# A decoder trunk on one core: pairs of gate/up blocks in seven products, in another form of the seven, and with a second pair in three of the four FFNs

## The chip, the cores and the metric

The kernel runs on one core of a Trainium2 chip. The metric is the device time of one execution in microseconds (us). The kernel before was timed three times: 978.38, 978.43 and 982.04 us, median 978.43.

## The reference, cut to what matters

Two layers work on x, 256 rows of 1024 numbers, in float32. Each layer has an FFN, a mixer (mLSTM beside attention to a memory in the first layer, dilated attention beside it in the second), and another FFN. Between the layers one projection makes keys and values that the second layer uses. The change is in the four FFNs:

```python
D_MODEL, SEQ, DEPTH, D_FF = 1024, 256, 2, 2816
def swiglu(h, w_gate, w_up, w_down):
    return (jax.nn.silu(h @ w_gate) * (h @ w_up)) @ w_down
...
    x = x + 0.5 * swiglu(rms_norm(x, ffn1_norm[layer]), ffn1_w_gate[layer], ffn1_w_up[layer], ffn1_w_down[layer])
    ...
    x = x + mix
    x = x + 0.5 * swiglu(rms_norm(x, ffn2_norm[layer]), ffn2_w_gate[layer], ffn2_w_up[layer], ffn2_w_down[layer])
```

The four FFNs are named here by layer and place: (0,1), (0,2), (1,1), (1,2).

## The kernel before, in words

**Numbers in two parts.** Every float32 operand of a matmul is split into a high and a low part: ScalarE (ACT) rounds it (`hi`), VectorE (DVE) subtracts that from it (`lo`). `mm3` (line 797) then issues three matmuls in place of one: x high by w low, x high by w high, x low by w high. So every unit of weights, a tile of 128x1024 numbers, costs a load of 512 KB, one rounding on ACT and one subtraction on DVE before TensorE (PE) can use it. `emit_unit` (line 658) issues that; the split weights go into a ring of 8 tiles each (`RING`, tags `hi` and `lo`), in the order in which PE uses them. Weights come in one packed array by the SP queue, into 6 buffers (`RAW`).

**An FFN in blocks.** The 2816 hidden columns are 11 blocks of 256. `gu(b, t)` makes gate and up of block b for the row half t (128 rows): 8 slices of 128 input channels, three matmuls of 128x512 each, so 24 matmuls in one PSUM bank (pool `mm`, two banks). `activated` (line 1030) makes silu on ACT and the product on DVE. For nearly all blocks `hidden_blocks` then transposes 32x32 squares on DVE, and `placed` (line 1066) sends the block through DRAM (`hd` out, `ht` back, one `ht` buffer) to put the squares where they belong, and splits it (`hhb`, `hlb`). `dn(b, t)` multiplies it with two units of w_down into the accumulators: 12 matmuls for each t.

**Pairs in seven products.** One pair of blocks, 5 and 6, is made in each FFN otherwise. Two row halves, two halves of the input channels and two blocks form a 2x2 product of matrices, which has eight block products; with sums of blocks on both sides seven are enough. `seventh(b, m)` (line 1163) issues product m: four channel slices, so 12 matmuls, with two units (k = 0 and 2). The sums of x are made once in an FFN (`sums`, line 1135) into the tiles `th` and `tl`. The sums of weights are made for every pair, in three buffers a, b and c for each k (`SLOTS`, line 75, `next_part`, line 620, `remade`, line 638): three subtractions or additions on DVE for each k, and two more as adding transfers, which a queue of GpSimd (POOL) issues and which add the next part of the weights into the buffer in SBUF. The results are put together from PSUM in the tiles `e` and `g`, with one copy on ACT and six sums on DVE of 128x512.

**The order of the work** is written out by hand in `PLANS` (line 49), one string for an FFN: g4 is `gu` of block 4, d2 is `dn` of block 2, 57 is product 5 of the pair that begins with block 7 (the product first, then the block), and p stands for a unit of the second mixer's output weights that is loaded, split and stored ahead of time in DRAM. Behind the string come `gu` of block 10 and the `dn` that the string left out, rows of t = 0 first: `gu(10,0)`, `dn` of the first block left, `gu(10,1)`, and so on (the end of `ffn_in`). In (0,1) and (1,1) the projection of the memory stands behind g4. PE runs in this order. The instructions of the other engines are put in order when the program is built, by a model of the engines (`_Model`, line 251; `until`, line 514): a chain's next step, or the split of the next unit, is written when the model's clock says that its inputs are ready. On the chip the engines' queues are then fixed, and each runs in order.

Of the kernel before, what the change touches and what calls it, by code (L numbers as in the profile page):

```python
# [12 lines left out]
ALU = mybir.AluOpType  # L13
# [27 lines left out]
def turned(layer, which, b):  # L41
# [20 lines left out]
SEVEN = {2: (2, 3), 5: (1, 0), 4: (3,), 3: (0,), 1: (0, 3), 6: (2, 0), 7: (1, 3)}  # L62
# [4 lines left out]
TWICE = ((0, 1), (0, 2), (1, 2))  # L67
# [5 lines left out]
PARTS = ((2, 0), (2, 2), (5, 0), (5, 2), (4, 0), (4, 2))  # L73
LAST = {"a": (1, 3, 4), "b": (6,), "c": (7,)}
SLOTS = {2: ("a", (0,), None), 5: ("b", (3,), None), 4: ("c", (2, 0), None),
         3: ("b", (1,), 5), 1: ("a", (), 5), 6: ("b", (), 3), 7: ("c", (), 4)}
# [33 lines left out]
def _stream():  # L110
# [26 lines left out]
    def ffn(layer, which):  # L137
# [11 lines left out]
        def st(b, m):  # L149
            for k in (0, 2):  # L150
                parts = tuple((layer, which, b, i, k) for i in SLOTS[m][1])
                units.append((("st", layer, which, b, m, k), ("parts", layer, parts, k, 2), 1024))
# [281 lines left out]
class _Kernel:  # L434
# [141 lines left out]


# [13 lines left out]
    def begin_parts(self, layer, which, plan, pool):  # L591

        self.partp, self.slots = pool, {}
        self.twice = (layer, which) in TWICE
        self.pairs = [(layer, which, s[1]) for s in plan if s[0] == "st" and s[2] == 2]
        self.todo = [(p, m, k) for p in range(len(self.pairs)) for m, k in PARTS]

    def before_part(self):

        p, m, k = self.todo[0]  # L600
        slot = SLOTS[m][0]
        p -= 2 if slot == "a" and self.twice else 1
        return [] if p < 0 else [(self.pairs[p], i, k) for i in LAST[slot]]

    def part_ready(self):
# [3 lines left out]
        p, m, k = self.todo[0]  # L609
        if self.index[("st",) + self.pairs[p] + (2, 0)] > self.next + EARLIER:  # L610
            return False
        if SLOTS[m][0] == "b" and not self.summed:
            return False
# [3 lines left out]
        return self.index[("st",) + self.pairs[p] + (m, k)] <= self.next + SOON or \  # L617
            self.model.clock["sync"] < self.now + LEAD

    def next_part(self):  # L620

        p, m, k = self.todo.pop(0)
        slot, parts, _ = SLOTS[m]
        if slot == "a" and (not self.twice or p % 2 == (self.pairs[p][:2] == (0, 1))):
            t = self.work.tile([P, 1024], F32, tag="mem", name="pa")
        else:
            t = self.partp.tile([P, 1024], F32, tag=f"p{slot}{k}", name=f"p{slot}{k}")
        pair = self.pairs[p]
        self.slots[pair, slot, k] = t
# [8 lines left out]
    def remade(self, pair, m, k):  # L638

        nc = self.nc  # L640
# [17 lines left out]
    def emit_unit(self):  # L658
# [12 lines left out]
        def steps(raw):  # L671
# [6 lines left out]
            if src[0] == "parts" and SLOTS[key[4]][2]:  # L678
                yield from self.wait(self.made[key[1:4], SLOTS[key[4]][2], key[5]])
# [30 lines left out]
        if src is not None and src[0] == "parts":  # L710
            slot = key[1:4], SLOTS[key[4]][0], key[5]
            while slot not in self.slots:
                self.finish(*[self.made[c] for c in self.before_part()])
                self.next_part()
            self.raw[i] = self.slots[slot]
# [28 lines left out]
    def unit_ready(self):  # L744
# [12 lines left out]
        if key[0] == "st" and SLOTS[key[4]][2]:  # L757
            c = self.made.get((key[1:4], SLOTS[key[4]][2], key[5]))
            if c is None or not c.done:
                return 1e9  # L760
        at = max(model.ready(raw[:, :self.units[i][2]]),
# [56 lines left out]
    def rms(self, src, out, later=LATER):  # L818
# [5 lines left out]
        for h in range(2):  # L824
            junk = self.work.tile([P, 512], BF16, tag="junk", name="junk")
# [188 lines left out]
    def ffn_in(self, layer, which, after, memory, fp):  # L1014
# [120 lines left out]
        def sums():  # L1135
# [4 lines left out]
            for t in range(2):  # L1140
                xs.append(fp.tile([P, NK, P], F32, tag=f"pb{2 * t}", name="xs"))
# [11 lines left out]
            for m in taken:  # L1153
                x, d = SEVEN[m], part[SEVEN[m][0]]
                if len(x) > 1:
                    d = self.work.tile([P, 4, P], F32, tag="sq", name="xd")
                    nc.vector.tensor_tensor(d, part[x[0]], part[x[1]], ALU.subtract)
                    yield
                yield from self.split(*taken[m], d)
# [864 lines left out]
```

## Time and profile before

| | |
|---|---|
| Profiled execution | 979.42 us, span 977.7 us, granted clock 1.0 |
| Median of the three timed runs | 978.43 us |
| PE, matmuls | 968.5 us busy (99%), 4631 instructions |
| PE, weight loads (PEld) | 805.4 us (82%) |
| DVE | 741.2 us (76%) |
| ACT | 580.0 us (59%) |
| POOL | 60.3 us (6%) |
| DMA | 220.79 MB, 226 GB/s; the adding transfers are 16 of 512 KB |

PE's busy share is made with modelled ends of pipelined matmuls, so it cannot tell how much of the time PE really works; the distance from one start to the next can. In the views, tiles are named as in the code: `gups` is the PSUM bank of a gate/up block or of a product, `acc` that of `dn`, `lo<-raw,hi` is the subtraction of a split, `pa`, `pb` and `pc` are the buffers of a pair's weights. Line 369 is the helper that issues every instruction of ACT, DVE, POOL and SP; line 787 is every matmul. The four FFNs lie at about 5 to 199, 319 to 498, 533 to 723 and 786 to 977 us of the span, the first mixer at 199 to 319, the keys and values at 498 to 533, and the second mixer at 723 to 786.

### The profile page before, as it was taken

To read this page: it belongs to the slowest core of one execution; us is meant where nothing else is said; L and a number is where in the kernel's file an instruction comes from. 1 tells how busy PE (TensorE), PEld (TensorE's weight loads), DVE (VectorE), ACT (ScalarE), POOL (GpSimd) and SP (SyncE) were. 2 spreads that over 40 slices of the span, in tenths; PEclk is the share of its full clock that TensorE was granted. 3 is DMA by queue.
4 is the path that set the end of the run, shared out by engine and by line. 5 is a ranking of instruction groups with operands and counts; after the bars stand their busy time and mean duration, and the time that the engine had idled before them with its cause. 6 is when DMAs were issued, how large, how long until landed. Compare 5 with 4: busy or idle time off the path is not lost.

```text
span 977.7 us, 13188 instructions
## 1 busy us (share of the span) xinstructions
PE 968.5 (99%) x4631; PEld 805.4 (82%) x4631; DVE 741.2 (76%) x1097; ACT 580.0 (59%) x921; POOL 60.3 (6%) x94
## 2 busy tenths in 40 slices
PE   9999999999999999999999999999999999999998
PEld 6787888899998888888888888888887788888887
DVE  5986985569886789965676897987676778689653
ACT  7766564477665655654476576575565585556541
POOL 0003000010010001000012002000012000000000
PEclk9999999999999999999999999999999999999999
DMA  9998398346355689588655889769658247965751
GB/s 357 321 331 251 89 313 267 99 148 226 122 193 197 224 257 264 166 258 290 215 180 186 273 276 304 210 241 349 236 194 298 104 172 253 332 169 186 257 181 44
DMA packets 84329, 220.79 MB, mean 226 GB/s; under 512 B 8044, under 2 KB 29480, under 8 KB 84264
## 3 DMA queue, kind: packets, MB, share of 16 engines
q1 hardware_dynamic: 81816, 211.54, 62.9%
q0 software_dynamic: 2304, 8.39, 4.7%
q8 instruction: 36, 0.59, 0.3%
q14 instruction: 29, 0.24, 0.1%
q10 hardware_dynamic: 144, 0.04, 0.0%
HBM read 203.14 MB, written 16.80 MB: 225 GB/s over the span
## 4 chain that ended last, share of the span: by engine, by line
PE 91%; DMA 3%; DVE 2%; ACT 2%; issue 1%; POOL 0%; SPq 0%; ACTq 0%; DVEq 0%; POOLq 0%
PE gups L787 45%; PE acc L787 23%; PE aps L787 8%; PE oacc L787 3%; PE kvps L787 3%; PE bqps L787 2%; DMA pc<-in_wts 1%; PE mkvps L787 1%; PE tps L794 1%; DMA raw<-in_wts 1%; ACT hi L369 1%; DVE s L369 1%; DVE lo L369 1%; PE po L787 1%; PE sc L787 1%
## 5 line engine op out<-in xcount | busy, mean ns | idle before, releaser
L369 DVE TENSOR_TENSOR lo<-raw,hi 128x1024 fp32r<-128x1024 f32 (+3 forms) x255 | 292.7, 1165 | 71.6 <-ACT hi L369 66.1
L369 ACT CAST hi<-raw 128x1024 fp32r<-128x1024 f32 (+3 forms) x255 | 251.5, 1007 | 79.0 <-PE gups L787 30.6
L787 PE MATMUL gups<-hi,xh 128*128 128x512 f32 x600 | 232.7, 390 | 0.0
L787 PE MATMUL gups<-lo,xh 128*128 128x512 f32 x600 | 232.6, 390 | 0.0
L787 PE MATMUL gups<-hi,xl 128*128 128x512 f32 x600 | 232.2, 389 | 0.0
L787 PEld LDWEIGHTS gups<-hi,xh 128*128 128x128 f32 x600 | 112.7, 188 | 24.2 <-ACT hi L369 1.1
L787 PEld LDWEIGHTS gups<-hi,xl 128*128 128x128 f32 x600 | 112.7, 188 | 23.7
L787 PEld LDWEIGHTS gups<-lo,xh 128*128 128x128 f32 x600 | 112.6, 188 | 23.2
L787 PE MATMUL acc<-lo,hhb 128*128 128x512 f32 x304 | 119.5, 393 | 0.0
L787 PE MATMUL acc<-hi,hlb 128*128 128x512 f32 x304 | 118.4, 390 | 0.0
L787 PE MATMUL acc<-hi,hhb 128*128 128x512 f32 x304 | 118.3, 389 | 0.0
L369 ACT ACTIVATE sil<-gups,rstd 128x256 f32<-128x256 f32 x80 | 37.7, 473 | 101.0 <-PE gups L787 90.7
L369 DVE SCALAR_TENSOR_TENSOR lo<-raw,gains,hi 128x512 fp32r<-128x512 f32 x128 | 88.7, 746 | 10.5 <-ACT hi L369 10.5
L369 ACT ACTIVATE hi<-raw,gains 128x512 fp32r<-128x512 f32 x128 | 83.3, 714 | 8.6 <-PE gups L787 4.2
L369 DVE SCALAR_TENSOR_TENSOR h<-gups,rstd,sil 128x256 f32<-128x256 f32 x80 | 38.1, 479 | 45.6 <-ACT sil L369 45.5
L787 PEld LDWEIGHTS acc<-hi,hlb 128*128 128x128 f32 x304 | 57.1, 188 | 12.0
L787 PEld LDWEIGHTS acc<-hi,hhb 128*128 128x128 f32 x304 | 57.1, 188 | 11.5
L787 PEld LDWEIGHTS acc<-lo,hhb 128*128 128x128 f32 x304 | 57.1, 188 | 11.4
L787 PE MATMUL aps<-lo,xh 128*128 128x384 f32 (+1 forms) x144 | 49.8, 346 | 0.0
L787 PE MATMUL aps<-hi,xl 128*128 128x384 f32 (+1 forms) x144 | 47.5, 330 | 0.0
L787 PE MATMUL aps<-hi,xh 128*128 128x384 f32 (+1 forms) x144 | 47.5, 330 | 0.0
L369 ACT CAST hhb<-ht 128x512 fp32r<-128x512 f32 x38 | 23.6, 620 | 40.1 <-DMA ht<-hd 40.0
(231 smaller groups left out, 1406.5 us busy)
## 6 DMA issues: line engine op xcount, KB each, us to landing
raw<-in_wts SPq DMA_DIRECT2D x278, 512.0 KB, 5.0
raw<-in_wts SPq DMA_DIRECT2D x32, 384.0 KB, 3.9
hd<-hb SPq DMA_DIRECT2D x38, 256.0 KB, 5.3
ht<-hd SPq DMA_DIRECT2D x38, 256.0 KB, 3.9
pa<-in_wts SPq DMA_DIRECT2D x8, 512.0 KB, 5.3
pb<-in_wts SPq DMA_DIRECT2D x8, 512.0 KB, 6.2
pc<-in_wts SPq DMA_DIRECT2D x8, 512.0 KB, 7.7
pc<-in_wts POOLq DMA_DIRECT2D x8, 512.0 KB, 8.0
```

Source lines behind the costliest of these rows:

```text
L369: call(out, *args, **kw)
L787: self.pe.matmul(out, lhsT=lhsT, rhs=rhs, start=start, stop=stop, skip_group_check=more)
L794: self.pe.transpose(out, in_, ident)
```

## The change

Three of the four FFNs make two pairs in seven products, blocks 5, 6 and 7, 8; (0,1) keeps one. The seven products take another form, in which one sum is built on the one before it. With w1 and w2 the weights of the first block of the pair (upper and lower half of the channels), w3 and w4 those of the second, the products' weights are w1; w3 - w1; w4 - (w3 - w1); w4 - w3; w2; w2 - (w4 - w3 + w1); w4. They are made in place, in four buffers a, b, c, d for each k, each loaded once: four subtractions on DVE for each k, no adding transfer. The tile a is w1, then w3 - w1, then w4 - (w3 - w1), so that each step waits until the split of the product before has read it. The results need one copy on ACT and five sums on DVE. The sums of x are four, not five. All four plans are new, and two "p" are left where there were four. To make room in SBUF, `junk` has one buffer and the warm-up tile shares it.

```diff
-    (0, 1): "g0 g1 g2 g3 d0 g4 d2 d1 25 55 d3 "
-            "45 35 15 d4 65 75 g7 g8 d6 g9 d7 d5",
-    (0, 2): "g0 g1 g2 d0 g3 g4 25 55 d1 d2 45 35 "
-            "15 65 d4 d3 75 g7 g8 d5 d6 d7 g9 p",
-    (1, 1): "g0 g1 g2 d0 g3 g4 d1 25 55 45 d2 d3 35 "
-            "p d4 15 65 75 g7 g8 p d6 d5 p g9 d7",
-    (1, 2): "g0 g1 g2 d0 g3 g4 d1 d2 25 55 d3 "
-            "45 35 15 65 d4 75 g7 g8 d5 g9 d6 d7",
+    (0, 1): "g0 g1 g2 d0 g3 g4 d2 d1 15 55 25 "
+            "65 d3 75 d4 45 35 g7 g8 d6 d5 g9 d7",
+    (0, 2): "g0 g1 g2 p d0 g3 d1 15 55 65 d2 25 75 d3 "
+            "45 35 g9 g4 d5 17 57 67 d6 77 27 47 37 d9 d4",
+    (1, 1): "g0 g2 g1 g3 d0 15 d1 55 65 d2 75 25 35 45 "
+            "g4 g9 17 p d3 d5 57 67 d4 77 27 47 d6 37 d9",
+    (1, 2): "g0 g1 g2 d0 g3 d1 15 55 65 d2 25 75 d3 45 "
+            "35 g9 g4 d5 17 57 67 d6 27 77 d4 47 37 d9",
...
-SEVEN = {2: (2, 3), 5: (1, 0), 4: (3,), 3: (0,), 1: (0, 3), 6: (2, 0), 7: (1, 3)}
+SEVEN = {1: 0, 2: 1, 4: 3}
...
-SLOTS = {2: ("a", (0,), None), 5: ("b", (3,), None), 4: ("c", (2, 0), None),
-         3: ("b", (1,), 5), 1: ("a", (), 5), 6: ("b", (), 3), 7: ("c", (), 4)}
+PARTS = (("a", 0), ("b", 1), ("c", 3), ("d", 2))
+LAST = {"a": (6, 2), "b": (7,), "c": (3,), "d": (4,)}
+SLOTS = {1: ("a", None), 5: ("a", 1), 6: ("a", 5), 2: ("d", None),
+         7: ("b", 6), 4: ("d", 2), 3: ("c", None)}
+NEEDS = {1: "ab", 5: "c", 6: "", 2: "d", 7: "", 4: "", 3: ""}
...
     def next_part(self):
...
-        self.nc.sync.dma_start(t, self.part_of(pair + (parts[0], k)))
-        for i in parts[1:]:
-            self.nc.gpsimd.dma_start(t, self.part_of(pair + (i, k)), accum_op=ALU.add)
+        self.nc.sync.dma_start(t, self.part_of(pair + (i, k)))
...
     def remade(self, pair, m, k):
-        a, b, c = (self.slots.get((pair, n, k)) for n in "abc")
-        if m == 5:
-            nc.vector.tensor_tensor(a, a, b, ALU.subtract)
-            yield
-            nc.gpsimd.dma_start(b, self.part_of(pair + (1, k)), accum_op=ALU.add)
-        elif m == 3:
-            nc.vector.tensor_tensor(b, b, a, ALU.add)
-        elif m == 4:
+        a, b, c, d = (self.slots.get((pair, n, k)) for n in "abcd")
+        if m in (2, 6):
             yield from self.wait(self.made[pair, 5, k])
-            nc.vector.tensor_tensor(c, c, a, ALU.subtract)
+        out, x, y = {1: (a, b, a), 5: (a, c, a), 6: (b, c, b), 2: (d, d, a)}.get(m, (None,) * 3)
+        if out is not None:
+            yield from self.when(x, y)
+            self.nc.vector.tensor_tensor(out, x, y, ALU.subtract)
...
+            if m == 1:
+                s["e"] = self.spawn(copied())
+            elif m == 2:
+                s["c11"] = self.holder[bank] = halved(None, None, b, 0)
+            elif m == 6:
+                s["u2"] = total(["e"], "gb", ps, "eb", "kn")
+            elif m == 7:
+                s["u3"] = total(["u2"], "ub", ps, "eb", "sq")
+                s["z"] = total(["u3"], "ub", s[5][1], "ub")
+                s["c22"] = halved("z", "ub", b + 1, 1)
+            elif m == 4:
+                s["y"] = total(["u3"], "eb", ps, "eb")
+                s["c21"] = halved("y", "eb", b, 1)
+                self.leaving(s["y"])
+            elif m == 3:
+                s["w"] = total(["z"], "gb", ps, "gb")
+                s["c12"] = self.holder[bank] = halved("w", "gb", b + 1, 0)
```

Here `total` is one sum of PSUM and SBUF on DVE, `halved` the activation and the transposes of one half block, and `copied` the copy on ACT. Products 2, 7, 4 and 3 run on in the bank of the product before (1, 6, 7 and 5), so each of them waits until that bank has been read.

More of the change, by code (lines that the diff above doesn't have):

```diff
@@ L575, in leave, with leaving, steps @@
         self.held[pool] -= n
+    def leaving(self, chain):
+        def steps():
+            yield from self.wait(chain)
+            self.leave("tp")
+        self.spawn(steps())
     def load_unit(self):
@@ L608, in part_ready @@
             return False
-        p, m, k = self.todo[0]
-        if self.index[("st",) + self.pairs[p] + (2, 0)] > self.next + EARLIER:
+        p, n, _, k = self.todo[0]
+        if self.index[("st",) + self.pairs[p] + (1, 0)] > self.next + EARLIER:
             return False
-        if SLOTS[m][0] == "b" and not self.summed:
+        if n == "d" and not self.summed:
             return False
@@ L677, in steps @@
                 yield
-            if src[0] == "parts" and SLOTS[key[4]][2]:
-                yield from self.wait(self.made[key[1:4], SLOTS[key[4]][2], key[5]])
+            if src[0] == "parts" and SLOTS[key[4]][1]:
+                yield from self.wait(self.made[key[1:4], SLOTS[key[4]][1], key[5]])
             gain, k, each = folded(key), src[3], width // src[4]
@@ L710, in emit_unit @@
         if src is not None and src[0] == "parts":
[L711 to L715, printed above, removed]
+            for n in NEEDS[key[4]]:
+                while (key[1:4], n, key[5]) not in self.slots:
+                    self.finish(*[self.made[c] for c in self.before_part()])
+                    self.next_part()
+            self.raw[i] = self.slots[key[1:4], SLOTS[key[4]][0], key[5]]
         if src is None:
@@ L1234, in c11, with total, steps @@
-            def c11():
-                nc.vector.tensor_tensor(s["e"], ps, s["e"], ALU.add)
-                self.leave("tp")
-                yield
-                yield from hidden_blocks(b, 0)(s["e"])
-            name, steps = {2: ("m2", m2), 5: ("h", h), 4: ("c21", c21), 3: ("c12", c12),
-                           1: ("f", f), 6: ("c22", c22), 7: ("c11", c11)}[m]
-            s[name] = self.spawn(steps())
-            if m in (4, 3):
-                self.holder[bank] = s[name]
+            def total(before, out, a, c, tag=None):
+                def steps():
+                    yield from self.wait(*[s[n] for n in before])
+                    if tag:
+                        s[out] = self.work.tile([P, 512], F32, tag=tag, name=out)
+                    nc.vector.tensor_tensor(s[out], a, s[c], ALU.add)
+                return self.spawn(steps())
@@ new lines, in copied, with halved, steps @@
+            def copied():
+                s["eb"] = self.work.tile([P, 512], F32, tag="kn", name="eb")
+                nc.scalar.copy(s["eb"], ps)
+                return
+                yield
+            def halved(before, a, *which):
+                def steps():
+                    if before:
+                        yield from self.wait(s[before])
+                        yield FREE
+                    yield from hidden_blocks(*which)(s[a] if before else ps)
+                return self.spawn(steps())
@@ new lines, in placing @@
+            def placing(i, *ends):
+                if all(e in s for e in ends):
+                    chains[i, 0] = chains[i, 1] = self.spawn(placed(i, [s[e] for e in ends]))
+            if m == 1:
[15 more added lines that the diff above has]
+                s["c12"] = self.holder[bank] = halved("w", "gb", b + 1, 0)
```

119 lines of the change are left out of this document (43 added, 76 removed).

## The prediction

> **What bounds the kernel now.** I read the page's head first, then the starts of TensorE's weight loads in time, the busy time by stretches, the waits of PE, and last single instructions of VectorE and the DMA issues.
>
> ```profile
> span 977.7 us, 13188 instructions
> PE 968.5 (99%) x4631; PEld 805.4 (82%) x4631; DVE 741.2 (76%) x1097; ACT 580.0 (59%) x921; POOL 60.3 (6%) x94
> ```
>
> PE is shown busy nearly all the time, but the ends of its matmuls are modelled. Starts are surer (start, length, both in us):
>
> ```profile
> 442.07 0.19 PEld L787 LDWEIGHTS acc<-hi,hlb 128*128 128x128 f32 x1
> 442.30 0.19 PEld L787 LDWEIGHTS acc<-lo,hhb 128*128 128x128 f32 x1
> 442.52 0.19 PEld L787 LDWEIGHTS acc<-hi,hhb 128*128 128x128 f32 x1
> 442.75 0.19 PEld L787 LDWEIGHTS acc<-hi,hlb 128*128 128x128 f32 x1
> ```
>
> Three steps take 0.68 us, so one matmul of 128x512 costs 0.227 us of PE's time. Is that so over whole FFNs? Columns: stretch, length, then busy us and count of PE, PEld, DVE, ACT, POOL.
>
> ```profile
> 325.00:350.00 25.00, 25.00 (x112) 20.71 (x111) 19.10 (x26) 14.14 (x18) 0.07 (x1) 1.00 0.76 264
> 5.00:199.00 194.00, 191.90 (x852) 157.61 (x852) 149.25 (x201) 117.46 (x182) 12.26 (x18) 1.00 0.76 254
> 319.00:498.00 179.00, 179.00 (x800) 148.09 (x800) 135.62 (x172) 101.99 (x138) 5.39 (x8) 1.00 0.73 233
> 533.00:723.00 190.00, 190.00 (x847) 157.19 (x846) 151.62 (x216) 118.78 (x178) 8.52 (x10) 1.00 0.78 260
> 786.00:977.00 191.00, 188.47 (x843) 156.00 (x841) 136.00 (x174) 97.73 (x132) 5.33 (x8) 1.00 0.61 204
> 319.00:357.00 38.00, 38.00 (x171) 31.45 (x171) 30.10 (x45) 23.72 (x38) 0.88 (x2) 1.00 0.72 237
> 97.00:121.00 24.00, 24.00 (x108) 19.87 (x107) 23.54 (x26) 13.21 (x17) 0.00 (x0) 1.00 0.31 88
> 357.00:406.00 49.00, 49.00 (x217) 40.57 (x217) 45.42 (x52) 31.01 (x38) 3.65 (x4) 1.00 0.77 230
> 739.00:786.00 47.00, 44.53 (x325) 33.99 (x324) 35.98 (x83) 28.68 (x70) 5.02 (x5) 1.00 0.52 199
> ```
>
> The first row holds 111 loads in 25.00 us, 0.225 each: no gap. The second to fifth are the FFNs (0,1), (0,2), (1,1), (1,2): 0.224 to 0.228 us for each load, at a granted clock of 1.00. The FFNs are bound by the number of matmuls. VectorE is 71% to 80% busy in them, ScalarE less.
>
> The Trainium skill, "Perfetto Trace Analysis", section "Identifying the Most-Contended Engine", says that matmul busy time misleads and that the busy share of the weight loads shows the headroom. By it the 82% above would leave 18%, and a matmul taken out would only become more waiting. The first row speaks against that reading: 20.71 of 25.00 us is 83% too, in a full stream, so 83% is what this matmul shape can show.
>
> The longest wait of PE for another engine is small:
>
> ```profile
> PE tpk L794 <- DVE kn L369: 1.8, 1, 1.8
> ```
>
> It stands in (0,1), behind the memory's projection.
>
> **The matmuls taken out.** Two plain blocks are 2 x 2 x 24 = 96 matmuls, a pair in seven products 84. Three more pairs save 3 x 12 = 36, and 36 x 0.227 = 8.2 us, all of it on the path as long as the split weights are there in time. The existing pairs keep their 84.
>
> **What VectorE pays.** A stretch of its instructions in time (start, length):
>
> ```profile
> 382.06 0.44 DVE L369 STREAM_TRANSPOSE hb<-h 128x256 f32<-128x256 f32 x1
> 382.43 1.18 DVE L369 TENSOR_TENSOR lo<-pc,hi 128x1024 fp32r<-128x1024 f32 x1
> ...
> 384.91 1.22 DVE L369 TENSOR_TENSOR pc<-pc,pa 128x1024 f32<-128x1024 f32 x1
> 386.05 0.68 DVE L369 TENSOR_TENSOR g<-gups,e 128x512 f32<-128x512 f32 x1
> 386.65 1.22 DVE L369 TENSOR_TENSOR lo<-pb,hi 128x1024 fp32r<-128x1024 f32 x1
> ...
> 403.51 0.47 DVE L369 SCALAR_TENSOR_TENSOR h<-gups,rstd,sil 128x256 f32<-128x256 f32 x1
> 403.90 1.21 DVE L369 TENSOR_TENSOR lo<-raw,hi 128x1024 fp32r<-128x1024 f32 x1
> ```
>
> A split or an in-place sum is recorded with 1.22 us, but the next one starts 1.14 us later (384.91 to 386.05); a sum of 128x512 takes a step of 0.60, the gated product 0.39, a transpose 0.37. I count in steps. A pair after has 14 splits and 8 in-place sums (25.1), 5 sums of results (3.0), 4 times product and transpose (3.0): 31.1 us, beside 84 x 0.227 = 19.1 us of PE. Two plain blocks have 8 splits and the same 4: 12.1. So a new pair puts 19.0 us on VectorE, and an existing one 2 in-place sums less one sum, 1.7. The sums of x lose one subtraction and one split, 1.2. (0,2) goes from 135.6 to 155.1 us in 176.3, 88%. (1,1) goes from 151.6 to 171.1, and to 168.8 as two "p" leave it, in 187.3, 90%. (1,2) goes from 136.0 to 155.5 in 188.3, 83%. On average it fits; ScalarE, with 6 roundings and a copy more, does with ease.
>
> A pair alone does not fit (31.1 beside 19.1), so the ring's lead must carry it. How long is the lead? The split of a pair's first unit and its first use:
>
> ```profile
> 365.61 1.22 DVE L369 TENSOR_TENSOR lo<-pa,hi 128x1024 fp32r<-128x1024 f32 x1 [0.44 <-ACT hi L369]
> ```
> ```profile
> 379.06 0.19 PEld L787 LDWEIGHTS gups<-lo,th 128*128 128x128 f32 x1
> ```
>
> It is 12.2 us from 366.83 to 379.06, and 357 to 406 us shows VectorE at 93% with PE never late. For (0,2) after, from product 1 of the first pair to product 3 of the second, PE has 2 x 84 + 2 x 48 (g9, g4) + 4 x 24 (d2, d3, d5, d6) = 360 matmuls, 81.7 us. VectorE has 2 x 28.1, 16 splits (18.2), 11 times product and transpose (8.4) and about 5 splits of hidden blocks (3.0): 85.8 us. A full ring of 8 units at the start, with the 4 sums between them, is 12 x 1.14 = 13.7 us done ahead. 85.8 against 81.7 + 13.7 = 95.4 leaves 9.6 us. Before that start the stretch 319 to 357 had 7.9 us of VectorE idle, so the ring can be full. (1,2) has d4 inside as well, (1,1) the memory's projection and two more d. I take no lateness here; the upper bound is in the rivals.
>
> The Trainium skill, "VectorE: DVE Perf Modes", section "The DRAIN you can't avoid", says that the next operation does not start until the pipeline has emptied, and that one which nothing holds starts earlier. The first half speaks against this change. By the recorded 1.22 us the 85.8 us would be 85.8 x 1.22 / 1.14 = 91.8, and 3.6 us would be left of the 9.6. The starts above overlap by 0.08 us, so the trace takes the steps' side, and the sum is the same by both.
>
> **The transfers that go.**
>
> ```profile
> pc<-in_wts POOLq DMA_DIRECT2D x8, 512.0 KB, 8.0
> pb<-in_wts POOLq DMA_DIRECT2D x8, 512.0 KB, 7.3
> hd<-hb SPq DMA_DIRECT2D x38, 256.0 KB, 5.3
> ht<-hd SPq DMA_DIRECT2D x38, 256.0 KB, 3.9
> ```
>
> The 16 adding transfers go, and with them 16 issues on POOL. No wait of PE hangs on them, so they bring 0. A pair's eight loads are as many as two plain blocks', so no new load appears; they now go behind SP's other issues, with 8 to 14 units of notice.
>
> **New waits of PE.** Products 2, 7, 4 and 3 run on in a bank that a copy or a sum must have read first, and all of PE's queue stands behind them. Between a product and the next one in its bank lie at least 12 matmuls, 2.7 us, beside 0.68 us for a sum (386.05). The tightest is "75 25 35" in (1,1): product 3 needs two sums behind product 7, 1.3 us, and two splits may stand ahead of them on VectorE, 2.3. That is 0.9 more than 2.7. I take 0, since the order of VectorE is built around such due times and PE waits for no `gups` sum now.
>
> **The way through DRAM at the end of (1,2).** Behind "47 37 d9" stand gu(10,0) and then dn(7,0): from the end of product 4 to dn(7,0) PE has 12 + 24 + 24 = 60 matmuls, 13.6 us. The last product of a pair before shows what its block needs:
>
> ```profile
> 421.19 0.68 DVE L369 TENSOR_TENSOR e<-gups,e 128x512 f32<-128x512 f32 x1
> ...
> 423.91 0.33 SPq L369 DMA_DIRECT2D hd<-hb  x1
> ...
> 434.29 0.62 ACT L369 CAST hhb<-ht 128x512 fp32r<-128x512 f32 x1 [0.38 <-DMA ht<-hd]
> ...
> 435.86 0.65 DVE L369 TENSOR_TENSOR hlb<-ht,hhb 128x512 fp32r<-128x512 f32 x1
> ```
>
> From the sum to the issue 2.7, to the rounding 10.4, to the end of the split 2.2: 15.3 us, 1.7 more than there is. With the median landings (5.3 + 3.9) in place of 10.4 it is 14.1, 0.5 more. In (0,2) and (1,1) d9, d4 or d6 stand between as well, 5.4 us more, which covers it. I take 0.8, between 0 and 2.3.
>
> **(0,1).** From 97 to 121 us VectorE was busy for 23.54 of 24.00. Its pair gets 1.7 us more. The last product's splits were this far ahead:
>
> ```profile
> 115.13 2.32 DVE L369 TENSOR_TENSOR lo<-pc,hi 128x1024 fp32r<-128x1024 f32 x2
> ```
> ```profile
> 118.67 0.19 PEld L787 LDWEIGHTS gups<-lo,th 128*128 128x128 f32 x1
> ```
>
> The first half was done at about 116.3 and used at 118.7, so 2.4 us of cover takes the 1.7. If the wait for `kn` (1.8) goes, PE comes that much earlier and the cover is short. I take 0.5, between -1.8 and 1.7.
>
> **The second mixer.** Two units of its output weights are no longer made ahead: two roundings and two splits (2.3 us of VectorE) come back into 739 to 786 us, where PE has gaps and VectorE is at 35.98 of 47.00, in a chain with ScalarE. Two pairs of 512 KB loads go for two single ones, so DMA does not suffer. I take 0.8, between 0 and 2.3.
>
> **The sum.** -8.2 + 0.8 + 0.5 + 0.8 = -6.1 us, from the profiled execution's 979.42 us to 973.3. That execution lies 1.0 above the median of the runs, 978.43, so the forecast is 972.3 us.
>
> **The rivals.** (a) VectorE becomes the bound. At the 93% of its densest stretch, 85.8 us of work takes 92.3. If only 5 us are ahead when the first pair of (0,2) starts, because the chain of in-place sums (split, sum, rounding, split) waits for ScalarE at each step, PE has 81.7 + 5 and is 5.6 us late, and about as much in (1,1) and (1,2): 972.3 + 3 x 5.6 = 989. For it speaks that each step of the chain must end before the next; against it, two units alternate, and the 12.2 us above. It makes the kernel slower than before by 0.5% from 3.7 us for each FFN, a lead under 7 us. (b) The covers fail at the three small places: 2.3 + 1.7 + 2.3 = 6.3 us, and 978.43 - 8.2 + 6.3 = 976.5 (977.4 with the bank of (1,1)). For it speaks that all three covers are thinner than 3 us. (c) Nothing is late and the wait for `kn` goes too: 978.43 - 8.2 - 1.8 = 968.4. (d) The saved matmuls become waiting, as the rule on weight loads has it: 978.4; the full streams speak against it. That the change does not take out what it says cannot well be: the plans fix 36 matmuls.
>
> **How the numbers follow.** A measurement of this kernel can tell about 0.5%, 4.9 us, from no change. The forecast's case, up to 4.9 us under before, has 0.50; (c) 0.12; (b) 0.22; (d) 0.03; (a) 0.13. Faster is 0.50 + 0.12, the same 0.22 + 0.03, slower 0.13. The range goes from just under (c), 968.0, over (b) to 980.0, and leaves (a) out.
>
> **What would show it.** Right: 4595 matmuls; still 0.227 us from load to load through both pairs; VectorE near 85% to 90% in (0,2) and (1,1) with PE not late; no adding transfers; starts of (0,2), (1,1) and (1,2) to their ends shorter by 2.7 us each. Wrong: PE's waits for `lo` inside the second pairs (case a), a gap ahead of dn(7,0) in (1,2), more gaps in 739 to 786 us, or in (0,1) at the products behind the memory.

## The result, and the profile after

The change makes the kernel slower: 989.38 us median of 4 runs (987.44 to 990.05), beside 978.4 us of the kernel before on the same chip. The ratio is 1.010, with a 95% interval of 1.0073 to 1.0127. The forecast was 972.3 us in a range of 968 to 980. The profiled execution took 989.23 us, with a span of 987.5 us, 9.8 more than before's 977.7. The head of its page (span, then busy time of each engine, then the granted clock in 40 slices):

```profile
span 987.5 us, 13069 instructions
PE 966.7 (98%) x4595; PEld 798.9 (81%) x4595; DVE 797.2 (81%) x1143; ACT 592.7 (60%) x931; POOL 49.6 (5%) x78
PEclk9999899999999999999999999999999999999999
```

The 36 matmuls are gone (4631 to 4595), and VectorE is 56 us busier. But PE's weight loads fill 81% of a longer span instead of 82% of a shorter one: PE waits more than it saved. The fifth slice (99 to 123 us) has a digit 8: the clock was not granted in full there.

To find the place, I cut both traces at the start of each stage's first matmul; the last stage ends with the last matmul. Lengths in us:

| stage | before | after | change | forecast |
|---|---|---|---|---|
| FFN (0,1) | 194.2 | 200.5 | +6.3 | +0.5 |
| first mixer | 119.6 | 119.7 | +0.1 | 0 |
| FFN (0,2) | 179.2 | 176.5 | -2.7 | -2.7 |
| keys and values | 35.6 | 35.7 | +0.1 | 0 |
| FFN (1,1) | 190.0 | 193.8 | +3.8 | -2.7 |
| second mixer | 72.7 | 76.6 | +3.9 | +0.8 |
| FFN (1,2) | 177.9 | 176.2 | -1.6 | -1.9 |

The changes add up to 9.9 us; the span grew by 9.8. The same stages by stretches of the kernel after (stretch, length, busy us and count of PE, PEld, DVE, ACT, POOL, then the granted clock, the DMA share and GB/s):

```profile
5.00:205.00 200.00, 194.19 (x851) 158.76 (x851) 150.07 (x200) 117.10 (x180) 11.38 (x14) 0.98 0.68 241
325.00:501.00 176.00, 176.00 (x787) 145.69 (x786) 153.15 (x189) 106.40 (x144) 2.03 (x5) 1.00 0.66 230
537.00:731.00 194.00, 189.70 (x836) 154.38 (x836) 167.81 (x225) 119.75 (x175) 5.19 (x6) 1.00 0.67 233
808.00:984.00 176.00, 175.48 (x782) 144.78 (x781) 145.83 (x179) 94.95 (x125) 0.87 (x2) 1.00 0.57 200
```

(0,2) is at 786 loads in 176 us, 0.224 each, with VectorE at 87% and no gap on PE: the new pair does there what it was forecast to do. (1,1) has 836 loads in 194 us, 0.232 each: PE is late there. In (0,1) it is 0.235, and the clock is 0.98.

**(0,1).** PE's weight loads around its longest wait (start, length, what it waited for):

```profile
92.64 0.19 PEld L785 LDWEIGHTS gups<-lo,th 128*128 128x128 f32 x1 [1.20 <-issue]
...
98.22 0.29 PEld L792 LDWEIGHTS tpk<-consts,kn 128*128 128x128 f32 x2 [5.05 <-DVE kn L369]
...
98.71 0.33 PEld L785 LDWEIGHTS gups<-hi,th 128*128 128x128 f32 x1
99.14 0.33 PEld L785 LDWEIGHTS gups<-hi,tl 128*128 128x128 f32 x1
99.56 0.33 PEld L785 LDWEIGHTS gups<-lo,th 128*128 128x128 f32 x1
```

Before, the same transposes of the memory keys `kn` waited like this:

```profile
94.44 0.54 PEld L794 LDWEIGHTS tpk<-consts,kn 128*128 128x128 f32 x4 [2.20 <-DVE kn L369]
```

Their wait grows from 2.2 us to 5.0, and 1.2 stand ahead of it. (The prediction's 1.8 is the same wait in the matmul's row; the weight load's row has the 2.2.) Behind the wait the matmuls start 0.43 us apart instead of 0.227: twelve of them, 0.20 lost with each, 2.4 us. Together 1.2 + 5.0 + 2.4 - 2.2 = 6.4 us, the stage's 6.3. VectorE's instructions ahead of `kn`:

```profile
79.29 1.22 DVE L369 TENSOR_TENSOR pa<-pb,pa 128x1024 f32<-128x1024 f32 x1
...
81.69 1.23 DVE L369 TENSOR_TENSOR pa<-pc,pa 128x1024 f32<-128x1024 f32 x1
84.31 0.48 DVE L369 TENSOR_SCALAR kn<-mkvps,memr 128x256 f32<-128x256 f32 x1 [1.40 <-ACT sq L369]
...
86.64 1.22 DVE L369 TENSOR_TENSOR pa<-pc,pa 128x1024 f32<-128x1024 f32 x1
...
92.04 0.48 DVE L369 TENSOR_SCALAR kn<-mkvps,memr 128x256 f32<-128x256 f32 x1 [1.78 <-ACT sq L369]
...
96.81 0.69 DVE L369 TENSOR_TENSOR hlb<-ht,hhb 128x512 fp32r<-128x512 f32 x1 [3.69 <-ACT hhb L369]
...
97.75 0.42 DVE L369 TENSOR_TENSOR kn<-kn,rp_r 128x256 f32<-128x256 f32 x1
```

And ScalarE's in the same time:

```profile
83.37 0.48 ACT L369 ACTIVATE vm<-mkvps,memr 128x256 f32<-128x256 f32 x1 [2.85 <-POOL memr L369]
...
91.10 0.48 ACT L369 ACTIVATE vm<-mkvps,memr 128x256 f32<-128x256 f32 x1 [3.12 <-POOL memr L369]
...
96.16 0.62 ACT L369 CAST hhb<-ht 128x512 fp32r<-128x512 f32 x1 [4.22 <-DMA ht<-hd]
```

The new sums in place (`pa<-pb,pa`, `pa<-pc,pa`) stand among the keys' few instructions, and three queues that keep their order stop one another: ScalarE waits for GpSimd's `memr`, VectorE for ScalarE, and the last step of the keys (`kn<-kn,rp_r`) stands behind a split `hlb` whose block comes back from DRAM late: the transfer into its single buffer `ht` is issued at 93.2, once the `hlb` before it, at 92.4, has read that buffer. GpSimd has the last step's input `rp_r` ready at 89.9, so the step stands in VectorE's queue for 7.9 us. Before, the same step stood ahead of the split:

```profile
93.98 0.75 DVE L369 TENSOR_TENSOR kn<-kn,rp_r 128x256 f32<-128x256 f32 x2
94.65 0.68 DVE L369 TENSOR_TENSOR hlb<-ht,hhb 128x512 fp32r<-128x512 f32 x1
```

**(1,1).** The densest stretch, and then PE's waits (waited for: us, times, longest):

```profile
581.00:608.00 27.00, 25.74 (x113) 20.64 (x111) 26.51 (x30) 18.20 (x24) 0.00 (x0) 1.00 0.48 165
```
```profile
PEld gups L785 <- DVE kn L369: 2.3, 1, 2.3
...
PEld gups L785 <- DVE gb L369: 1.7, 1, 1.7
...
PEld gups L785 <- DVE h L369: 0.9, 1, 0.9
...
PEld gups L785 <- DVE tl L369: 0.8, 1, 0.8
```

From 581 to 608 us VectorE is busy for 26.51 of 27.00. PE's waits over 0.4 us in this stage add up to 7.2. In the first pair they are for `gb` (1.7), `tl` (0.8) and `ub` (0.5); three of 0.5 to 0.9 stand at plain blocks and the memory's projection around it. One more, 2.3 us, stands at 644: the block behind the memory keys needs a bank that the keys' instruction must read first. In the second pair there is none. What stands ahead of `gb`, for which product 7 waits at 608:

```profile
600.59 2.35 DVE L369 TENSOR_TENSOR lo<-pb,hi 128x1024 fp32r<-128x1024 f32 x2
...
606.50 1.22 DVE L369 TENSOR_TENSOR pd<-pd,pa 128x1024 f32<-128x1024 f32 x1
607.64 0.68 DVE L369 TENSOR_TENSOR gb<-gups,eb 128x512 f32<-128x512 f32 x1
```

Product 6, which `gb` reads, ends at about 601.3. Six splits and sums of 128x1024 run in VectorE's queue from 600.6 to 607.6, without a gap, before `gb` has its turn.

**The second mixer.** Its two largest waits after, and the same two before:

```profile
PEld oacc L785 <- DVE xl L369: 3.4, 3, 2.8
...
PEld tpq L792 <- issue: 1.9, 1, 1.9
```
```profile
PEld tpq L794 <- PE tpp L794: 0.9, 1, 0.9
...
PEld oacc L787 <- DVE xl L369: 0.5, 1, 0.5
```

These two groups alone grew by 3.9 us.

**(1,2).** A single wait, ahead of the last product dn(7,0), for the block that comes back through DRAM:

```profile
961.42 0.19 PEld L785 LDWEIGHTS acc<-lo,hhb 128*128 128x128 f32 x1 [0.94 <-ACT hhb L369]
...
962.15 0.19 PEld L785 LDWEIGHTS acc<-hi,hlb 128*128 128x128 f32 x1 [0.43 <-DVE hlb L369]
```

0.9 + 0.4 = 1.3 us, at the place that was forecast with 0.8.

### The profile page after: what moved, and what is told of

Read it like the earlier page. It is cut to its first block, busy times and chain, and to the rows that moved or that the text cites. A ratio compares the mean times of both kernels' runs of the same rounds, so it can differ in the third digit from the quotient of the medians.

```text
span 987.5 us, 13069 instructions
## 1 busy us (share of the span) xinstructions
PE 966.7 (98%) x4595; PEld 798.9 (81%) x4595; DVE 797.2 (81%) x1143; ACT 592.7 (60%) x931; POOL 49.6 (5%) x78
## 4 chain that ended last, share of the span: by engine, by line
PE 73%; DVE 12%; DMA 6%; ACT 4%; issue 4%; POOL 1%; SPq 0%; DVEq 0%; ACTq 0%
PE gups L785 34%; PE acc L785 19%; DVE lo L369 6%; PE aps L785 6%; PE oacc L785 4%; PE kvps L785 3%; DMA ht<-hd 2%; DMA raw<-in_wts 2%; PE bqps L785 2%; ACT hi L369 1%; PE mkvps L785 1%; DMA kept<-vs 1%; PE tps L792 1%; DMA hd<-hb 1%; DVE hlb L369 1%
## 5 line engine op out<-in xcount | busy, mean ns | idle before, releaser
L369 DVE TENSOR_TENSOR lo<-raw,hi 128x1024 fp32r<-128x1024 f32 (+3 forms) x239 | 271.9, 1158 | 45.8 <-ACT hi L369 42.7
L369 ACT CAST hi<-raw 128x1024 fp32r<-128x1024 f32 (+3 forms) x239 | 232.9, 1002 | 50.7 <-PE gups L785 19.3
L785 PE MATMUL gups<-lo,xh 128*128 128x512 f32 x540 | 210.2, 392 | 2.8 <-DVE kn L369 1.9
L785 PE MATMUL gups<-hi,xh 128*128 128x512 f32 x540 | 209.5, 390 | 0.0
L785 PE MATMUL gups<-hi,xl 128*128 128x512 f32 x540 | 209.2, 390 | 0.0
L785 PE MATMUL acc<-lo,hhb 128*128 128x512 f32 x304 | 119.6, 393 | 0.5 <-ACT hhb L369 0.5
L785 PEld LDWEIGHTS gups<-hi,xh 128*128 128x128 f32 x540 | 101.4, 188 | 22.0 <-ACT hi L369 1.4
L785 PE MATMUL gups<-lo,th 128*128 128x512 f32 x136 | 54.2, 398 | 2.2 <-DVE gb L369 1.3
L369 DVE TENSOR_TENSOR lo<-pa,hi 128x1024 fp32r<-128x1024 f32 x42 | 51.1, 1216 | 5.3 <-ACT hi L369 4.9
L785 PE MATMUL gups<-hi,tl 128*128 128x512 f32 x136 | 53.8, 396 | 0.3 <-DVE tl L369 0.3
L785 PE MATMUL gups<-hi,th 128*128 128x512 f32 x136 | 53.7, 395 | 0.0
```

Of the source, the lines that this page charges most:

```text
L369: call(out, *args, **kw)
L785: self.pe.matmul(out, lhsT=lhsT, rhs=rhs, start=start, stop=stop, skip_group_check=more)
```

## The experiments

All kernels are the kernel after with one edit, but for e7, which is the kernel before with one. Changes of the stages against before, in us; "one run" is the time of a single profiled execution:

| kernel | time | (0,1) | (0,2) | (1,1) | second mixer | (1,2) |
|---|---|---|---|---|---|---|
| after | 989.38, 4 runs | +6.3 | -2.7 | +3.8 | +3.9 | -1.6 |
| e1 | 989.71, one run | +5.6 | -2.7 | +3.4 | +3.9 | -0.9 |
| e2 | 993.63, one run | +5.0 | +3.6 | +6.3 | 0.0 | -1.4 |
| e3 | 992.46, one run | +5.7 | -2.7 | +7.6 | +3.9 | -1.8 |
| e4 | 987.97, one run | +5.8 | +1.5 | +1.0 | 0.0 | 0.0 |
| e5 | 976.43, one run | -3.0 | -2.7 | +5.2 | +0.1 | -2.7 |
| e6 | 992.26, one run | +4.4 | -2.7 | +6.4 | +5.5 | -1.8 |
| e7 | 985.67, one run | +5.4 | 0.0 | 0.0 | +0.2 | 0.0 |
| e8 | 986.92, one run | +5.2 | -2.7 | +2.3 | +3.9 | -1.7 |
| e10 | 984.47, one run | +1.9 | -2.7 | +3.7 | +3.9 | -1.9 |
| f1 | 972.30, 4 runs | -2.9 | -2.7 | +0.1 | +2.5 | -2.7 |
| f2 | 978.31, 10 runs | -2.3 | -2.7 | +5.8 | +0.3 | -2.7 |
| f3 | 973.04, 4 runs | -2.6 | -2.7 | +0.9 | +0.2 | -2.7 |
| f4 | 976.51, one run | -2.1 | -2.7 | +2.4 | +1.0 | -2.7 |

How far can one trace be trusted? (0,1) has the plan of the kernel after in e2, e3, e4, e6 and e8 too, and reads +4.4 to +6.3 with it; (1,1) has it in e1, e2, e5 and e10, and reads +3.4 to +6.3. Part of that is the clock, as the last section shows. So a difference of less than 2 us in these two stages says little by itself, and there the waits must be read. (0,2), (1,2) and the mixer repeat within 0.5, but for one mixer (e6).

**e1: a plain block between the memory keys and the pair of (0,1); (0,2)'s order in (1,2).**

```
-    (0, 1): "... d2 d1 15 55 25 65 d3 75 d4 45 35 g7 g8 d6 d5 g9 d7"
+    (0, 1): "... d2 d1 g7 15 55 25 65 d3 75 d4 45 35 g8 d6 d5 g9 d7"
-    (1, 2): "... d5 17 57 67 d6 27 77 d4 47 37 d9"
+    (1, 2): "... d5 17 57 67 d6 77 27 47 37 d9 d4"
```

> The changed kernel with two plans altered. In (0,1) the plain block g7 is moved from behind the pair to between the memory's projection and the pair. In (1,2) the order of (0,2) is used, so that d9 and d4 stand behind product 4 and not ahead of it. Theory: in (0,1) the pair's splits and in-place sums and the normalisation of the memory's keys share VectorE's queue at the same moment, and PE waits 5.0 us for the keys and then runs at half the clock; with 10.9 us of plain matmuls between them both have room, the stage from 5 to 205.6 us gets 5 to 7 us shorter and the clock share returns to 1.000. In (1,2) the wait of 1.3 us ahead of dn(7,0) goes. Together 6 to 8 us less than the changed kernel: 981 to 983. Rival (the chain of in-place sums makes VectorE the bound wherever a pair stands): (0,1) keeps at least 4 of its 6.3 us, and the time stays at 986 or more.

989.71 us. The keys' wait is gone, but (0,1) gains only 0.7, since another takes its place:

```profile
PEld acc L781 <- ACT hhb L365: 6.8, 1, 6.8
```

It stands at 147 us: "35 g8 d6" leaves only g8's 48 matmuls, 10.9 us, between the pair's last product and d6, whose block has to go through DRAM, 15.3 us by the prediction's rows. So the keys' wait is a matter of place, and moving one block moved the lateness on. The expected 981 to 983 us didn't come. The rival named 986 or more and got it, but for another reason than its chain of sums. In (1,2) the wait ahead of dn(7,0) went, and one of 2.0 came at d9.

**e2: the two missing units of the second mixer made at the end of (0,2).**

```
-    (0, 2): "... 77 27 47 37 d9 d4"
+    (0, 2): "... 77 27 47 37 d9 d4 p p"
```

> The changed kernel with two more units of the second mixer's output weights split ahead of time, at the end of (0,2), so that there are four as in the kernel before. Theory: the 3.8 us that the second mixer got longer (72.7 to 76.5 us from its first matmul to the first of (1,2)) come from the two units that VectorE and ScalarE split there again; the mixer goes back to 72.5 to 73.5 us and (0,2) grows by less than 0.5. Time 985.5 to 986.5. Rival (the mixer is longer because of the order of the loads and of the ring ahead of it, or of the one junk buffer): it stays at 75.5 us or more, and the time at 988 to 990.

The mixer is back at 72.7 us, so its 3.9 us come from the two units alone. But (0,2), expected to pay less than 0.5, pays 6.3 for them, over half of it ahead of its last product dn(8,0):

```profile
PEld acc L781 <- DVE lo L365: 3.4, 1, 3.4
```

**e3: (1,1)'s first pair behind the memory keys.**

```
-    (1, 1): "g0 g2 g1 g3 d0 15 d1 55 65 d2 75 25 35 45 g4 g9 17 ..."
+    (1, 1): "g0 g2 g1 g3 d0 g4 d1 15 55 65 d2 75 25 35 45 g9 17 ..."
```

> The changed kernel with the first pair of (1,1) moved behind g4, the memory's projection and d1, where the kernel before has its pair. Theory: (1,1) lost its 6.5 us because the sums of x (with the gain, about 17 operations of 0.6 to 0.7 us on VectorE) and the first pair's splits fall into the same 45 us, so that the ring has no lead when the pair starts; later the sums are done and the lead is there: (1,1) from 193.8 to 188 to 190 us, time 983.5 to 985.5. It may keep a wait for the memory's keys of up to 2 us. Rival (two pairs are too much for VectorE in (1,1) wherever they stand): the same waits move to the second pair, (1,1) stays at 192 us or more.

(1,1) becomes longer, 197.5 us. The waits moved with the work: 1.4 us at 634, 2.0 at 658, 3.3 at 666, with VectorE busy for 14.12 of 15.00 us from 640 to 655. The rival held: that the pair only stood too early is not the cause.

**e4: the nested form alone, with as many pairs and in the places of before.** (0,2), (1,1) and (1,2) get one pair each, behind g4, in the order "15 55 65 .. 25 75 .. 45 35", and their plain blocks and "p" back.

> The new form of the seven products with one pair in each FFN, with the plan of the changed kernel in (0,1), plans like those before in the others, and four units ahead. No matmul is saved. Theory: the form itself costs nothing outside (0,1); (0,2), (1,1), (1,2) and the second mixer are within 0.7 us of the kernel before (179.3, 190.0, 177.9, 72.7), and (0,1) keeps its 6.3: time 984 to 986. Rival (the in-place chain is the bound): each of the three FFNs with one pair is 2 us or more longer than before, time 990 or more.

Outside (0,1) the form costs less than the rival's 2 us, but in two stages more than the 0.7 expected: 1.5 us in (0,2) (one wait between products 1 and 5, for a gated product `h` on VectorE), 1.0 in (1,1), nothing in (1,2), nothing in the mixer. (0,1) keeps its 5.8. So the chain of sums in place is not a bound wherever a pair stands.

**e5: other places in (0,1) and (1,2).** The pair of (0,1) stands behind g7, ahead of d6 and d5 there are g8, g9 and d7, and the two missing "p" are in (0,1):

```
+    (0, 1): "... d2 d1 g7 15 55 25 65 d3 75 d4 45 35 g8 p g9 d7 p d6 d5"
+    (1, 2): "... d5 17 57 67 d6 77 27 47 d4 37 d9"
```

> The changed kernel with three places altered at once, each in a stage of its own. (0,1): g7 ahead of the pair, and behind the pair g8, g9, d7 before d6 and d5, so that the blocks of the pair have 27 us for their way through DRAM and not the 11 of the run with g8 alone; in the same FFN two units of the second mixer's output weights are made ahead, behind g8 and d7. (1,2): d4 between products 4 and 3 of the second pair. Theory: no wait for the memory's keys, none ahead of d6: (0,1) at 194 to 195.5 us (200.5 in the changed kernel); second mixer at 72.5 to 73 (76.6); (1,2) at 175 to 175.5 (176.2); (1,1) unchanged at 193.8. Span 977 to 979, time 978.5 to 980.5. Rival for (0,1) (the pair's form has too little room there anyway): it stays above 197.

976.43 us (the kernel before took 980.91 beside it), 13 less than after, with the same number of products. That is below the 978.5 to 980.5 expected, since (0,1) gained more. (0,1) goes from +6.3 to -3.0, the mixer to +0.1 and (1,2) to -2.7. In (0,1) no wait over 1 us is left. What stays is (1,1), with 195.2: its plan is that of after, and behind the bank's wait of 2.3 us seven matmuls start 0.43 us apart, which makes the 1.4 more than after's 193.8.

**e6: the sums of x in (1,1) on GpSimd** (four sums of `xh` and `xl` and their products with the gain).

> The changed kernel with 8 operations of (1,1) moved from VectorE to GpSimd: the four additions that put x together again from its two parts and the four multiplications with the gain, 128x512 each. Nothing else. Theory (VectorE's load ahead of the first pair of (1,1) is what makes PE late): about 5 us of VectorE go out of the 45 us ahead of the pair, and (1,1) goes from 193.8 to between 188 and 191 us. Rival 1 (the waits come from the chain of the pair or from the memory's keys, not from the load): (1,1) stays at 193 or more. Rival 2 (GpSimd is so slow beside a busy VectorE that the sums come later than before): (1,1) gets longer than 195.

(1,1) grows to 196.4. The waits of the first pair shrink, but a new group is larger than all of them:

```profile
PEld gups L781 <- DVE h L365: 7.2, 2, 5.9
```

A row of GpSimd and one of VectorE say why:

```profile
551.04 1.74 POOL L365 TENSOR_TENSOR xs<-xh,xl 128x512 f32<-128x512 f32 x1
```
```profile
548.45 9.44 DVE L365 SCALAR_TENSOR_TENSOR lo<-raw,gains,hi 128x512 fp32r<-128x512 f32 x6
```

Rival 2 held. Six splits with the gain take 9.44 us, 1.57 each, while GpSimd's eight instructions run (548.3 to 560.1, 1.47 each); two of them after that take 1.41, 0.7 each. VectorE loses what it was to be spared. (The mixer's +5.5 has a drop of the clock in it, at 780 us.) The Trainium skill, "SBUF — State Buffer", section "SBUF: two separate sides", says that GpSimd and an operation of VectorE with two inputs from SBUF share a pair of ports, and that whichever starts first holds it for its whole instruction. These rows agree: about one split runs for each instruction of GpSimd.

**e7: the kernel before with one buffer for the squares of the statistics,** which the change has too:

```
-            junk = self.work.tile([P, 512], BF16, tag="junk", name="junk")
+            junk = self.work.tile([P, 512], BF16, tag="junk", bufs=1, name="junk")
```

> The kernel before with one thing of the change: the junk tile has one buffer and the warm-up shares it. Theory: the single buffer plays no part; every stage within 0.5 us of the kernel before, time 978 to 979.5. Rival (the single buffer separates the two statistics of the memory and so makes its keys late): in (0,1) the wait for the memory's keys grows from 2.2 towards 5 us, and (0,1) from 194.2 to 197 us or more.

985.67 us, all of it in (0,1), but not at the keys:

```profile
PEld acc L787 <- ACT hhb L369: 4.5, 2, 3.0
...
PEld tpk L794 <- DVE kn L369: 2.2, 1, 2.2
```

The keys' wait is before's 2.2, so the rival failed; but the theory that the buffer plays no part failed too. The planner, which orders each engine's queue by modelled times, has put the issues on SP in another order, and the blocks come late through DRAM for d6 (1.5 us at 144) and d7 (3.0 at 164, with a drop of the clock behind it). So one buffer less can cost 5 us in (0,1) by itself, in another place than in the kernel after: its 5.0 at the keys are not explained by it.

**e8: no sums in place in (1,1).** The sixteen sums of 128x1024 in (1,1) are left out, and the splits are of the parts as they came.

> The changed kernel without the 16 in-place subtractions of weights in (1,1); the products there use the buffers as loaded, so this part of the computation is left out. Theory (VectorE's load): 18 us less on VectorE in (1,1); the waits at the first pair go, and (1,1) comes down to 187.5 to 189.5 us, what is left being the memory's keys. Rival (waits that have nothing to do with the load, such as the order of the queue or the bank that the memory's keys hold): (1,1) stays above 191.5.

The waits of the first pair and around it, 4.9 us, are gone, as the theory has it. But the stage, 192.2, is only 1.5 shorter and lies in the rival's range. Left is the bank behind the keys (2.5), and behind it the clock drops (1.4); a transpose behind the second pair waits 1.1. Together that is the 5.0 by which this run still misses the forecast:

```profile
PEld gups L781 <- DVE kn L365: 2.5, 1, 2.5
```

**e10: no sums in place in (0,1).** The eight sums of its pair are left out (the expectation counts six). (A first run of this edit, e9, took 3432 us: its matmuls start 0.84 us apart instead of 0.227 in the whole program, at a recorded clock of 1.00. It tells nothing of the edit.)

> The kernel after without the sums in place of (0,1)'s pair (six of 128x1024 on VectorE; that part of the computation is left out, the splits are of the parts as they came). Theory A (the memory keys' long wait of 5.0 us in (0,1) comes from work on VectorE that stands ahead of them): the wait falls to the 2.2 us of before or less, the clock doesn't drop behind it, (0,1) 193 to 196. Theory B (it comes from the order of the in-order queues: the transfer by DRAM and the single buffers behind the statistics, whichever engine has work): the wait stays at 4 us or more, (0,1) 198 to 201.

```profile
PEld tpk L788 <- DVE kn L365: 2.7, 1, 2.7
```

5.0 and 1.2 us of waiting become 2.7, and (0,1) is 196.1, 4.4 less than after. So the sums among the keys' instructions make most of it. Theory A was wrong in two points: the wait stays above 2.2, and the clock did drop behind 2.7 us, for seven matmuls, 1.4 us. With 2.7 + 1.4 - 2.2 = 1.9 the stage is accounted for. The order that theory B names is still there: the last step of the keys (95.0) again stands behind the `hlb` (94.1) of a block from DRAM, only earlier.

**f1: e5, and one pair in (1,1),** behind the keys as in e4, with one "p".

```
+    (1, 1): "g0 g1 g2 d0 g3 g4 d1 15 55 65 d2 25 75 d3 45 35 d4 g7 g8 p d6 d5 g9 d7"
```

> The kernel with the places of e5_places in (0,1) and (1,2), and in (1,1) the one pair (5 and 6) behind the memory keys that e4_form_alone had there, with one of the mixer's pieces instead of three. Theory (the dense stretch of VectorE in (1,1), sums of x with the gain and the splits of two pairs, is what costs there): e4's stage of 191.0 less its waits around the pieces, 190 to 191.5 in place of e5's 195.2, the other stages as in e5 within 0.5: 976.4 - 5.2 + 0.5 = 971 to 973 us. Rival (the pieces made in (0,1) or the later stages shift when (1,1) changes, so stages don't add): mixer B or (1,2) longer by 2 or more, 974 to 977 us.

972.30 us (972.18 to 974.30) beside 979.62 of the kernel before: a ratio of 0.9924, 95% interval 0.9903 to 0.9945. This version beats both kernels. Its profiled execution is the slowest of the four, with a granted clock of 0.84 from 770 to 780 us. The other three have a clock of 1.00 and are 2.0 us shorter, so most of the 2.5 in the mixer belongs to that execution.

**f2: e5, and both pairs in (1,1) with more ahead of them.**

```
+    (1, 1): "g0 g1 g2 d0 g3 g9 d1 15 55 65 d2 25 75 d3 45 35 g4 d9 p 17 d5 57 67 77 27 47 d6 37 d4"
```

> As f1_one_pair_11, but (1,1) keeps both pairs: a plain block (the ninth) and a last product ahead of the first pair, the memory keys and two last products between the pairs. Theory (VectorE is behind only because the sums of x with the gain, the first pair's splits and sums in place and the memory keys come at once): with 5 to 11 us more ahead of the first pair and two last products to cover the keys, (1,1) takes 187.5 to 190, less than one pair's 190 to 191.5, and the kernel 968.5 to 972 us. Rival (VectorE has too little idle time in the whole stage for two pairs and the gain's sums together, wherever they stand): waits of 1 to 3 us at three places or more, in both pairs, (1,1) 193 to 196, 974 to 978 us.

The stage came out in the rival's range, but the first pair runs without a wait; the second one has them all:

```profile
PEld gups L781 <- DVE lo L365: 5.0, 3, 4.1
...
PEld gups L781 <- DVE gb L365: 1.6, 1, 1.6
```

(1,1) takes 195.8 and the kernel 978.31 us (ratio 0.9983, 0.9972 to 0.9995). In all three places tried (the kernel after, e3, f2) two pairs in (1,1) cost more than they save. In f2 the wait for `gb` is in part the plan's own: "67 77" puts product 7 right behind product 6, whose bank it runs on in, with no matmul between. Product 6 ends at 666.6, `gb` starts at 667.1 and ends at 667.8, and only then can PE go on.

**f3: f1 with its "p" ahead of the pair's last product** ("45 p 35 d4 g7 g8 d6").

> f1_one_pair_11 with the mixer's piece in (1,1) ahead of the pair's last product instead of behind two plain blocks. Theory (the second mixer needs its last prepared piece soon enough; in f1 it came too late and two waits of 1.0 and 1.1 us stood at 774 us): mixer B 72.7 to 73.5, (1,1) 190 to 191, the kernel 970 to 971.5. Rival (the waits in the second mixer don't depend on where the piece is made, but on how the mixer's own chains fall): mixer B 74.5 to 76, the kernel 972 to 973.5.

The mixer's stage is 72.9, but the time, 973.04 us (972.88 to 974.52; ratio 0.9935, 0.9915 to 0.9955), is not below f1's. The waits at 774 us, for which the "p" was moved, stand in the kernel before as well (0.8 and 1.2 at 778). The place of the "p" decides nothing that could be seen here.

**f4: f2 without the sums in place of (1,1).** They are sixteen, 19.7 us of VectorE; the expectation counts twelve and 14.7.

> f2_plain_ahead_11 without the sums in place of both pairs in (1,1) (twelve of 128x1024 on VectorE, some 14.7 us; that part of the computation is left out). Theory (VectorE's load in this stage is what delays: with the gain's sums, the keys and two pairs it is behind between 640 and 700): f2's waits of 1.6, 0.7 and 4.1 us in the second pair fall to under 1.0 together, (1,1) 188.5 to 190. Rival (the waits come from the chain of the second pair, each split behind the product ahead of it, or from transfers that land late, not from VectorE's load): at least 3 us of them stay, (1,1) 192 to 195.

(1,1) takes 192.4, 3.4 less than f2, 2.4 more than before. PE's two largest waits now:

```profile
PEld tph L788 <- DVE h L365: 2.9, 2, 2.7
...
PEld gups L781 <- DVE gb L365: 2.1, 1, 2.1
```

The stage lies in the rival's range, but not for the rival's reason: the waits for splits (4.8) are gone, so the load made them, and with them a drop of the clock that f2 has at 679. What is left goes with order. `gb` has f2's "67 77" to wait for (product 6 ends at 667.4), and then one more split (667.2 to 668.4) that was queued ahead of it; `h`, at 708.8, stands behind two roundings on ScalarE and four splits of later blocks. What a plan with matmuls between 67 and 77, and an order with `gb` and `h` first, would give back wasn't tried.

## Why the prediction was wrong, point by point

- **The matmuls taken out, right.** 4595 are left, at 0.227 us while PE isn't late. (0,2) shows the whole 2.7 us, and so do (1,2) and (0,2) in e5.
- **(0,2): "I take no lateness here", right there.** VectorE is 87% busy (88% forecast) and PE has no wait. The balance with the ring's lead holds for a FFN with two plain blocks between its pairs.
- **The same step for (1,1) failed, by 6.5 us.** I had worked the balance for (0,2) alone, and let (1,1) pass because "the memory's projection and two more d" stand inside. What I left out is that in (1,1) the sums of x have a gain to be multiplied in, and that they and their splits, from 550 us on, come just when the splits of the first pair are due: its product 1 starts at 587, 50 us into the stage. The average was right (167.81 us of VectorE forecast as 168.8); the stretch was not, with 26.51 of 27.00. e8 takes the sums in place away, and the waits of the first pair and around it go, 4.9 of 7.2 us; e3 and f2 move the pair, and the waits move on; f1 takes one pair out, and no wait over 0.3 us is left. So these waits come from VectorE's work in this stage. That its load alone would have to go is not shown: e8 also shortens the queue, its stage gained only 1.5 us, and by f2 and f4 the order costs some as well. The other 2.3 us of waits are the keys' bank.
- **"New waits of PE: I take 0" failed in (1,1).** I had priced product 3's wait for its two sums at 0.9 with two splits ahead of them and still put it at nothing; it came with 0.5 (`ub`). The larger one is product 7's, 1.7, with six splits and sums ahead of `gb` where I had allowed for two. And I had looked at products of one pair only, not at the plain block behind the keys, 2.3.
- **(0,1): "I take 0.5, between -1.8 and 1.7" failed, by 5.8 us,** the second largest miss. The step looked at the end of the pair (115 to 119 us), where 2.4 us of cover did take the 1.7. It did not look at the beginning, where the pair's sums in place now come among the memory keys, and the keys' last step behind a block from DRAM, in queues that keep their order and with single buffers. e10 shows the sums as most of it, e1 and e5 that another place avoids it. A bound "by the nearest rows" holds only at the place of those rows.
- **The second mixer: "0.8, between 0 and 2.3" was mis-sized: 3.9.** e2 shows that the two units are the cause. I priced them as 2.3 us of VectorE, but PE waits longer where that work comes back; the two groups shown above grew by 3.9.
- **(1,2): 0.8 for the way through DRAM, right in place and nearly in size** (1.3, within 0 to 2.3). e5's "47 d4 37 d9" puts 24 more matmuls between, and the wait is gone.
- **The adding transfers: 0, not contradicted.** No run here has them back with the new form.
- **Rival (a) gave 989, the time that came, but not for its reason.** It had (0,2), (1,1) and (1,2) late by 5.6 each. Two of the three weren't late at all or by 1.3; its mechanism, VectorE behind in a pair, is seen in (1,1) alone, and (0,1) and the mixer gave the rest. That its number came is luck. e4 speaks against its "chain of in-place sums" as a bound everywhere.

What stays open: whether in (0,1) the order of the keys' last step and the `hlb` alone makes the 0.5 us by which e10's wait is longer than before's (no run changes that order by itself), what holds the second mixer's chain in detail, and what in the kernel after the one buffer of e7 costs (no run has that kernel with two).

## What to carry to other kernels

When an engine pays for what another is spared, work the balance out for every stage that gets the work, on its densest stretch, and look at what else comes due there; forecast averages of 88% and 90% hid nothing in (0,2) and 6.5 us in (1,1). Before adding work to an in-order queue, look at both ends of its stretch for a short chain over several engines (here the memory keys) that will now stand among it. Before giving such work up, try its place: the same products gave 989 us in one order and 976 in another, and 972 with one pair fewer.

## What the runs showed of the hardware

PE's clock can drop behind a short wait: after 2.3 us (e5, in (1,1)), 2.5 (e8) and 2.7 (e10) seven matmuls start 0.43 us apart, after 5.0 (the kernel after) twelve. 2.2 us in the kernel before left it alone, and so did the 2.3 in (1,1) of the kernel after, the very wait that brought the drop in e5. A drop adds 1.4 to 2.4 us to the wait itself, and an equal wait can cost nothing or that sum. The granted clock of the kernel after shows it (stretch, then as above):

```profile
95.00:100.00 5.00, 1.78 (x6) 1.49 (x7) 3.19 (x5) 3.84 (x5) 1.99 (x2) 0.71 0.07 21
100.00:105.00 5.00, 5.00 (x15) 3.94 (x14) 5.00 (x6) 1.42 (x3) 0.17 (x1) 0.61 0.00 0
```

The Trainium skill, "TensorE: Matmul & The Clock Gate", section "HAM oscillation — how this bites in real kernels", gives idle gaps over about 3.4 us as what brings the clock down. The 5.0 us agree; the drops behind 2.3 to 2.7 us don't fit a bound on the length of one gap.

The traces show why equal waits differ. The clock changes only at the ends of steps of 3.413 us that are counted through the whole program: in the kernel after it is full from 4.92 to 97.08 us, 27 steps, and then low for two, to 103.90. A drop goes with how little PE worked within one such step. A wait of 2.2 us in the kernel before leaves it 1.63 us of its step, and the clock stays; the 2.3 in e5 leaves 1.51, and the next step has half the clock (stretch, then as above):

```profile
91.14:94.55 3.41, 1.63 (x8) 1.04 (x7) 3.41 (x5) 1.26 (x2) 2.40 (x2) 1.00 0.49 159
```
```profile
632.48:635.90 3.42, 1.51 (x7) 0.96 (x6) 2.56 (x4) 3.42 (x7) 0.00 (x0) 1.00 1.04 420
635.90:639.31 3.41, 3.41 (x10) 2.66 (x9) 3.34 (x6) 1.10 (x2) 1.51 (x2) 0.50 0.94 359
```

The same wait in the kernel after lies across two steps, which keep 2.70 and 2.20 us, and nothing drops. In the FFNs of all traces but e9's, at full clock, every step with 1.54 us of recorded matmul time or less was followed by a drop, and none with 1.63 or more; in a mixer one drop (f1) came behind 1.84.
